# RWKV products of a hybrid layer regrouped by tile shape: y in two blocks, the solve's heads alternating over two PSUM tiles, the low-rank products as 64-row tiles

## The chip, the core and the metric

The kernel runs on one core of a Trainium2 chip. The metric is device time in microseconds (us) from one execution of the whole program. Three runs of the kernel before took 2709.77, 2721.66 and 2725.01 us; their median is 2721.66 us.

The engines are named as in the profile: PE multiplies matrices, PEld is its weight load, DVE is the vector engine, ACT the scalar engine, POOL the third elementwise engine, SP issues most transfers. PE multiplies a stationary operand (the weights, K rows by M columns) with a moving one (K rows by N columns). A product that uses fewer than 128 rows or columns of the array addresses a part of it, a tile of 64x128, 128x64 or 64x64 (rows x columns of the array). This tile shape is what the change is about.

## What is computed

One step of a layer over 1024 prompt tokens and 8 sample sequences, all in float32: a half-step SwiGLU feed-forward, two token mixers side by side (S5 and RWKV-7), a gated merge, a second half-step feed-forward and a final norm. The change lies in the RWKV-7 mixer, whose recurrence is, for each of 8 heads with a 64 x 64 state:

```
w = -softplus(-(w0 + tanh(wd) @ w2)) - 0.5;  decay = exp(-exp(w))
a = sigmoid(a0 + ad @ a2);  g = sigmoid(gd) @ g2          # low-rank: w2, a2 are 64 x 512
sa = einsum('bhij,bhj->bhi', s, a_t)
s  = s * decay + sa * b_t + v_t * k_t;   y_t = einsum('bhij,bhj->bhi', s, r_t)
```

wd and ad are 64 features each, and stand in one 128-row tile (wad): wd in rows 0 to 63, ad in rows 64 to 127.

## The kernel before, in words

Activations lie with features in the partitions and the 1032 columns (tokens, then samples) in three chunks of 344. A dense product (`dense`, L144 to L155) is split into three: high weights by high input (L152), high by low (L153), low by high (L154), each 128 x 128 weights and 344 columns. These make up most of PE's work in the whole kernel; a *dense pass* below is one of them. Products of plain float32 operands (the RWKV ones) are run by the chip as two passes each, so 8 products show as x16 in the profile; transposes (L160) as one.

The RWKV mixer (`rw_run`, L1076) takes 16 steps: two halves of the heads, and for each 8 blocks of 128 tokens. A step handles two head pairs of two 64-token chunks, thus four pieces j of two heads each. Head 0 of a pair sits on partitions 0 to 63, head 1 on 64 to 127 (`HS`). The stages of several steps overlap:

- `rw_prep`, five steps ahead: the low-rank products (L846), decay products on DVE, norms of the keys (L869). Here w2 and a2 stand in a zero-padded weight tile (`wa2`, two blocks of 512 columns, cleared on POOL at L776), so that one 128-row product per block takes only its own 64 rows of wad. Four products write one PSUM tile `sv`.
- `rw_solve`, three steps ahead: products of rows a, r with rows b, k (L917), 64 rows by 128 columns, four for head 0 into one `sv` tile, then four for head 1 into another. ACT and DVE read them out; then a 15-step substitution on DVE and a round trip through DRAM give the inverses of 16 x 16 blocks.
- `rw_quad`, one step ahead: transposes (L160), the bonus (L985) and five sets of 64x64 products (L997) that make the whole inverse.
- `rw_chain`: the recurrence itself. For each chunk c: L1023 (128x64), a copy on ACT, L1028 (64x64), two copies on ACT, L1033 (128x64), then DVE's new state (L1037), and the outputs y: for each of two pieces, two products of full height (L1041, 128x64), then two of 64 rows (L1043, 64x64) that are added to them.
- `rw_tail`: group norm and gate (L1064, 64x64; L1071, 128x128).

Pool `sv` has two PSUM slots, `qd` two, `ch` and `y` one each. A new tile of a pool waits until the tile that held its slot has been read. Beside these stages stand dense products of lower priority: the last three RWKV tiles and the gate tiles (`gate_tiles`, 72 dense passes each), which fill PE between the RWKV products. A scheduler merges them at build time into one fixed order on each engine, and each engine keeps that order. I call the piece of PE's order from the first L846 to the last L1071 *the stage*; after it come the rest of the gate tiles, the S5 gate (`glu_tile`), and the sample step (`rw_sample_vectors`, L1116, whose low-rank products are L1134, in pool `sm` with one slot).

Of the kernel before, what the change touches and what calls it, by code (L numbers as in the profile page):

```python
# [22 lines left out]
P = 128  # L23
D = 1024
KD = D // P
NP = 1024            # prompt tokens
NB = 8               # sample sequences
T = NP + NB          # columns
CH = T // 3          # column chunk (one PSUM bank)
LP = NP - 2 * CH     # prompt columns in the last chunk  # L30
# [11 lines left out]
def host_consts():  # L42
    """Identity, ones and masks; they depend on shapes alone."""
    r = np.arange(P)[:, None]
    c = np.arange(P)[None, :]
    c64 = np.arange(64)[None, :]
    m = r % 64
    up = lambda k: (((c64 >> k) - (m >> k)) == 1) & ((c64 >> (k + 1)) == (m >> (k + 1)))
    d = {
        "ident": r == c,  # L50
        "ones": np.ones((P, P)),
        "bones": r // 64 == c // 64,
        "su": r % 64 < c64,
        "ui": r % 64 <= c64,
        "up": np.concatenate([up(4), up(5)], axis=1),
        "i64": m == c64,
    }
    cf = np.concatenate([d[n].astype(np.float32) for n, _ in CF], axis=1)
    return np.ascontiguousarray(cf)
# [6 lines left out]
class Net:  # L66
# [51 lines left out]
    def split(self, hi, lo, src):  # L118
        """hi + lo = src exactly, both with 12 significant bits."""
# [4 lines left out]
    def wload(self, *srcs, pool=None):  # L124
        """One weight unit of at most 1024 columns as (hi, lo); srcs stack along the middle."""
# [14 lines left out]
    def wcols(self, w, j, n=P):  # L140
        """Column block j of w[(k p), f] as [p, k, n]."""
        return self.wload(w[:, j * n:(j + 1) * n].rearrange("(k p) f -> p k f", p=P))

    def dense(self, terms, c, cols=None):  # L144
        """terms: list of (wh, wl, xh, xl) with [K,128] and [K,cols]; returns PSUM."""
# [11 lines left out]
    def tr(self, out, in_):  # L157
        """out[M, K] = in_[K, M] transposed through the tensor engine."""
# [31 lines left out]
    def ada_steps(self, strips, pool):  # L190
        """Modulation columns of up to four 512-wide strips, side by side in the array; one step per k."""
# [24 lines left out]
    def norm_params(self, q, ks):  # L216
        """a = g (1 + scale) of norm q for the feature tiles ks."""
# [16 lines left out]
    def rsqrt(self, pt, scale, eps_col, pool, floor=None, n=CH, m=P, tmp=None):  # L234
        """1/sqrt(scale * pt + eps) (or of max(pt, floor)), refined by one Newton step."""
# [30 lines left out]
    def norm_apply(self, h, q, c, rs, xh, xl, pool):  # L266
        """One chunk of xh + xl = modulate(rmsnorm(h)) for norm q."""
# [23 lines left out]
    def norm_steps(self, h, q, pool, params=True):  # L291
        """scale(c, tag) and apply(c, xh, xl) of norm q, to be called chunk by chunk."""
# [9 lines left out]
    def resid(self, h, hin, pt, g, d, c):  # L302
        """h[d] = hin[d] + pt * g over one chunk."""
# [12 lines left out]
    def ffn(self, h, q, w1, w3, w2, xh, xl, gp, groups, hooks=None, wp2=None, wide=None):  # L316
        """h += gate * (silu(x w1) * (x w3)) w2 for the hidden tiles of some groups.

        wide: the order of a group's steps: "Hc.e" the hidden products of a chunk, "Oc" its output.
        """  # L320
# [39 lines left out]
    def load_x(self, h, g, pool):  # L360
        """Token tiles 3 g .. 3 g + 2 (the last group ends with the samples), transposed into h."""
# [24 lines left out]
    def final_out(self, h, c, pool, gf):  # L386
        """rmsnorm(h) * g_final for one chunk of tokens, turned token-major first."""
# [28 lines left out]
    def exp_small(self, out, x, pool, n):  # L416
        """exp(x) by range reduction and a polynomial (fp32 accuracy)."""
# [42 lines left out]
    def cmul(self, ore, oim, are, aim, bre, bim, t1, eng=None):  # L460
        """(ore, oim) = a * b; outputs must not alias inputs."""
# [9 lines left out]
    def s5_prep(self, sp):  # L471
        """Discretised parameters; the wide ones go to DRAM scratch by quarters of 8 groups."""
# [9 lines left out]
        # [(g2 n), gp] views of lam_re, lam_im and log_dt  # L482
# [30 lines left out]
        # k = (lam_bar - 1) / lam  # L513
# [15 lines left out]
        # powers lam_bar^tau, tau = 0..8, and the same reversed (7 - s)  # L529
# [12 lines left out]
        # bb[(g2 n), gp, c]  # L542
# [7 lines left out]
        # C as [(g2 n), gp, c]  # L550
# [14 lines left out]
        for g in range(16):  # L565
            nc.sync.dma_start(self.sK[:, 2 * g:2 * g + 2, 0:112], zer)
            # lam^(7-s) bb -> transposed
# [12 lines left out]
            # C lam^tau, sign folded into the imaginary part  # L580
# [6 lines left out]
            # K_tau[c, c']  # L587
# [10 lines left out]
            # e^{i 8 ang q}, q = 0..127  # L598
# [13 lines left out]
    def s5_quarter(self, qd, X, Xs, us, Z, h0, zs, dbc, pool, tag):  # L612
# [53 lines left out]
        # sample states: lam_bar h0 + bb u  # L666
# [8 lines left out]
        # outputs; one PSUM bank per parity of the group, as the parities use different row tiles  # L675
# [30 lines left out]
    def s5_mix(self, X, usT, zout, pool, tag="mm"):  # L706
        """X [128 q, 32 g, 8 s, 16 c] chunk-major inputs, usT [128, 4, 8]; zout(ct, tile) gets z transposed."""
# [12 lines left out]
        # sample rows, once as the first and once as the last token of a chunk  # L720
# [29 lines left out]
        # states out  # L750
# [11 lines left out]
    def rw_init(self, rows, keep, tag):  # L762
        """Per-feature vectors and low-rank weights."""
# [11 lines left out]
        wa2 = self.t(keep, [P, 2, 512], "rw_wa2")  # L775
        nc.gpsimd.memset(wa2, 0.0)  # L776
        nc.sync.dma_start(wa2[0:64, 0, :], i["rwkv_w2"])
        nc.sync.dma_start(wa2[64:128, 1, :], i["rwkv_a2"])
# [4 lines left out]
    def rw_clear(self, pool):  # L783
        """Zeros around the diagonal blocks of the inverses' scratches."""
# [8 lines left out]
    def rw_lora(self, wad, gd):  # L793
        """wad rows: 64 of wd, 64 of ad; gd: 128 rows (mixed, [128, T])."""
# [6 lines left out]
    def inv_half(x, h):  # L801
        """[64, 4, 64] view of head h; the heads of a scratch lie 4160 apart."""
# [3 lines left out]
    def inv_diag(x):  # L806
        """[32, 16, 16] view of the diagonal blocks of a scratch."""
        return x.rearrange("(q r) -> q r", r=1040)[:, 0:1024].rearrange("q (t s) -> q t s", s=64)[:, :, 0:16]

    def rw_decay(self, sw, tmp, r, exps):  # L810
        """exps(fm, fp, r): r (1 - t)^2 and r (1 + t)^2 are exp(-y), exp(y) for y = e^-0.5 sw and t = tanh(y/2)."""
# [3 lines left out]
        # 1 / (1 - t^2) = (1 + t^2)(1 + t^4)(1 + t^8)(1 + t^16), t < 0.295  # L815
# [13 lines left out]
    def rw_part(n):  # L829
        """Tokens of step n, and its two head pairs with their columns in the step's tiles."""  # L830
# [3 lines left out]
    def rw_prep(self, n, pool):  # L834
        """Decay products, normalised keys and the like for two chunks each of two head pairs."""
# [7 lines left out]
        pt = self.t(self.pp, [P, 2, 256], "sv")  # L843
        for p, ts in pairs:
            for z in range(2):
                nc.tensor.matmul(pt[:, z, ts], self.wa2[:, z, p * P:(p + 1) * P], self.wad[:, tok], start=True, stop=True)  # L846
        sw, b = new("sw"), new("pb", 2)
        for p, ts in pairs:
            nc.scalar.activation(sw[:, ts], pt[:, 0, ts], AF.Sigmoid, bias=col("w0", p))
        for p, ts in pairs:  # L850
            nc.scalar.activation(b[:, ts], pt[:, 1, ts], AF.Sigmoid, bias=col("a0", p))
# [27 lines left out]
    def rw_solve(self, n, q, pool):  # L879
        """Products of the rows a, r with the rows b, k of four chunks, and the inverses of I - A's 16-blocks.  # L880

        The state is carried without the decay of its last chunk, which a and r take up.  Head h's feature rows
        sit on its own half of the partitions with b's token rows; k's and v's token rows sit on the other.
        """
# [29 lines left out]
        for h, (hs, op) in enumerate(zip(HS, opp)):  # L914
            pm = self.t(self.pp, [P, 4, 2, 64], "sv")
            for j in range(4):
                nc.tensor.matmul(pm[:, j].rearrange("p a b -> p (a b)"), bk[hs, j],  # L917
                                 R[hs, j].rearrange("p a b -> p (a b)"), start=True, stop=True)
            nc.scalar.copy(At[hs], pm[hs, :, 0])
# [3 lines left out]
        # the 16 x 16 diagonal blocks, one per partition  # L923
# [28 lines left out]
    def rw_quad(self, n, q, sv, pool):  # L952
        """b, k and v with their tokens in the rows, the bonus, and the whole inverse."""
# [6 lines left out]
        # v of each head in the columns of the other half, next to columns that nothing reads  # L960
# [18 lines left out]
        # bonus  # L979
# [8 lines left out]
        # (I - A)^-1 = X P1 P2 from the inverse X of the diagonal blocks, with P1 = I + A1 X and P2 = I + A2 X P1 for  # L988
        # the blocks A1 next to them and A2 below; Y is the transpose
# [19 lines left out]
    def rw_chain(self, m, nxt, pool):  # L1009
        """The recurrence over two chunks of two head pairs; the state after each goes into the next one's operand."""  # L1010
# [6 lines left out]
        for c in range(2):  # L1017
# [21 lines left out]
            for a, j in js:  # L1039
                for h, hs, op in hh:  # L1040
                    mm(py[hs, 0, j], W[:, j, 1, h], SUV[:, j, h, 1], start=True, stop=False)  # L1041
                for h, hs, op in hh:
                    mm(py[hs, 0, j], rs[hs, j], SUV[hs, j, h, 0], start=False, stop=True)  # L1043
        return py

    def rw_tail(self, n, py, bon, pool):
        """Group norm, bonus and output gate of a step; py has the tokens of both heads in its rows."""
# [28 lines left out]
    def rw_run(self, pool):  # L1076
        """All head pairs, two at a time, two chunks a step, the stages of successive steps overlapped."""
# [38 lines left out]
    def rw_sample_vectors(self, pool, tag="sv"):  # L1116
        """Vectors of the samples' step, as [128, 8 samples, 4 head pairs] and as rows (sample, head) in DRAM."""
# [476 lines left out]
```

## Time and profile before

| | |
|---|---|
| runs | 2709.77, 2721.66, 2725.01 us |
| profiled execution | 2725.0 us, the span alone (the slowest of the three runs) |
| PE, PEld, DVE, ACT, POOL busy | 97%, 90%, 56%, 30%, 17% of the span |
| the stage, 1183 to 1649 us | PE busy 447.7, DVE busy 403.1 of 466 us |
| 1286 to 1552 us, its even part | PE busy 258.2, DVE busy 243.6 of 266 us |

How to read it: PE's busy time is modelled from start times, and a pass's record is longer than its place in the stream (a dense pass has a record of 0.32 us and the next one starts 0.16 us later). So what a product costs on PE is read from the differences of start times in the list in order of time. Rows of that list merge equal passes that follow each other: start, time from first start to last end, engine, line, operation, tiles, rows*columns of the array, operand shape, count.

### The profile page before, as it was taken

To read this page: it belongs to the slowest core of one execution; us is meant where nothing else is said; L and a number is where in the kernel's file an instruction comes from. 1 tells how busy PE (TensorE), PEld (TensorE's weight loads), DVE (VectorE), ACT (ScalarE), POOL (GpSimd) and SP (SyncE) were. 2 spreads that over 40 slices of the span, in tenths; PEclk is the share of its full clock that TensorE was granted. 3 is DMA by queue.
4 is the path that set the end of the run, shared out by engine and by line. 5 is a ranking of instruction groups with operands and counts; after the bars stand their busy time and mean duration, and the time that the engine had idled before them with its cause. 6 is when DMAs were issued, how large, how long until landed. Compare 5 with 4: busy or idle time off the path is not lost. (4 is left out here: it accounts for less than half of the span.)

```text
span 2725.0 us, 46727 instructions
## 1 busy us (share of the span) xinstructions
PE 2635.2 (97%) x18175; PEld 2454.6 (90%) x18175; DVE 1521.9 (56%) x4140; ACT 804.8 (30%) x1574; POOL 464.3 (17%) x1123
## 2 busy tenths in 40 slices
PE   7999999999999899999999999899899999999998
PEld 4799999999999898888888889899899999999998
DVE  4533446555555715559989973667854444444435
ACT  4311111111113412256666743221521111111113
POOL 2200003776002300022322210410410000000001
PEclk9999999999999997889999999899899999999999
DMA  7443341222122212333333327543211111111101
GB/s 258 114 139 111 123 128 55 63 66 69 60 68 94 79 54 84 88 105 81 82 79 79 86 64 212 171 120 105 66 55 47 47 47 47 47 47 47 48 24 63
DMA packets 301041, 233.20 MB, mean 86 GB/s; under 512 B 77778, under 2 KB 264947, under 8 KB 300820
## 3 DMA queue, kind: packets, MB, share of 16 engines
q1 hardware_dynamic: 298002, 224.04, 27.9%
q0 software_dynamic: 1920, 5.27, 0.5%
q8 instruction: 143, 2.34, 0.4%
q10 hardware_dynamic: 898, 0.91, 0.1%
q14 instruction: 78, 0.64, 0.1%
HBM read 186.23 MB, written 43.92 MB: 84 GB/s over the span
## 5 line engine op out<-in xcount | busy, mean ns | idle before, releaser
L152 PE MATMUL mm<-xa,wh 128*128 128x344 f32 x2064 | 677.9, 330 | 8.2 <-ACT xa L282 5.6
L154 PE MATMUL mm<-xa,wl 128*128 128x344 f32 x2064 | 674.2, 327 | 3.0 <-DVE wl L122 3.0
L153 PE MATMUL mm<-xb,wh 128*128 128x344 f32 x1848 | 604.0, 327 | 6.2 <-DVE xb L279 2.4
L153 PE MATMUL mm<-xa,wh 128*128 128x344 f32 x1368 | 442.6, 324 | 3.9 <-DVE xa L279 3.1
L121 ACT CAST wh<-wr 128x1024 fp32r<-128x1024 f32 (+1 forms) x190 | 194.6, 1030 | 792.4 <-PE mm L153 695.7
L152 PEld LDWEIGHTS mm<-xa,wh 128*128 128x128 f32 x2064 | 393.7, 191 | 38.5 <-issue 17.3
L307 DVE SCALAR_TENSOR_TENSOR h<-mm,modG,h 128x344 f32<-128x344 f32 (+1 forms) x624 | 351.6, 571 | 126.0 <-PE mm L154 108.7
L154 PEld LDWEIGHTS mm<-xa,wl 128*128 128x128 f32 x2064 | 393.8, 191 | 9.9 <-DVE wl L122 3.5
L152 PE MATMUL mm<-xb,wh 128*128 128x344 f32 x1152 | 371.7, 324 | 5.2 <-ACT xb L121 2.8
L154 PE MATMUL mm<-xb,wl 128*128 128x344 f32 x1152 | 371.1, 323 | 0.0
L153 PEld LDWEIGHTS mm<-xb,wh 128*128 128x128 f32 x1848 | 352.2, 191 | 16.1 <-DVE xb L279 4.7
L122 DVE TENSOR_TENSOR wl<-wr,wh 128x1024 fp32r<-128x1024 f32 (+1 forms) x190 | 230.7, 1214 | 223.3 <-ACT wh L121 218.6
L152 PE MATMUL mm<-gh,wh 128*128 128x344 f32 x1056 | 340.1, 322 | 2.1 <-DVE h L307 1.7
L153 PE MATMUL mm<-gl,wh 128*128 128x344 f32 x1056 | 337.9, 320 | 0.0
L154 PE MATMUL mm<-gh,wl 128*128 128x344 f32 x1056 | 337.9, 320 | 0.0
L328 DVE TENSOR_TENSOR silu<-silu,mm 128x344 f32<-128x344 f32 x132 | 67.5, 511 | 473.8 <-PE mm L154 424.6
L153 PEld LDWEIGHTS mm<-xa,wh 128*128 128x128 f32 x1368 | 260.9, 191 | 5.8 <-DVE xa L279 4.0
L152 PEld LDWEIGHTS mm<-xb,wh 128*128 128x128 f32 x1152 | 219.2, 191 | 7.2 <-ACT xb L282 3.2
L154 PEld LDWEIGHTS mm<-xb,wl 128*128 128x128 f32 x1152 | 219.2, 190 | 0.0
L152 PEld LDWEIGHTS mm<-gh,wh 128*128 128x128 f32 x1056 | 198.7, 188 | 7.5 <-ACT wh L121 2.5
L154 PEld LDWEIGHTS mm<-gh,wl 128*128 128x128 f32 x1056 | 198.7, 188 | 0.2
L153 PEld LDWEIGHTS mm<-gl,wh 128*128 128x128 f32 x1056 | 198.7, 188 | 0.1
(506 smaller groups left out, 3344.9 us busy)
## 6 DMA issues: line engine op xcount, KB each, us to landing
wr<-ffn_w SPq DMA_DIRECT2D x132, 512.0 KB
wada<-w_ada SPq DMA_DIRECT2D x144, 256.0 KB
wr<-w_in SPq DMA_DIRECT2D x34, 512.0 KB
sGate<-gate SPq DMA_DIRECT2D x48, 172.0 KB
gate<-sGate SPq DMA_DIRECT2D x48, 172.0 KB
sMix<-gate SPq DMA_DIRECT2D x36, 172.0 KB
sH<-h SPq DMA_DIRECT2D x8, 516.0 KB
h<-sH SPq DMA_DIRECT2D x8, 516.0 KB
```

Source lines behind the costliest of these rows:

```text
L121: nc.scalar.copy(hi, src)
L122: nc.vector.tensor_sub(lo, src, hi.bitcast(F32))
L152: nc.tensor.matmul(pt, wh, xh[:, cols], start=q == 0, stop=False)
L153: nc.tensor.matmul(pt, wh, xl[:, cols], start=False, stop=False)
L154: nc.tensor.matmul(pt, wl, xh[:, cols], start=False, stop=q == last)
L307: nc.vector.scalar_tensor_tensor(h[d][:, c0:c0 + np_], pt[:, :np_], g[:, d, 0:1], hin[d][:, c0:c0 + np_], op0=ALU.mult, op1=ALU.add)
L328: nc.vector.tensor_mul(s, s, p3)
```

## The change

Three regroupings, and comments removed (which shifts line numbers: L846 becomes L845, L869 L868, L917 L916, L1043 L1045, L1134 L1136).

- y: for each chunk first all four products of full height (L1041), then all four of 64 rows. Only the very first of a step sets the start flag; the others find their columns cleared.
- The solve: two `sv` tiles are taken at once, and the products alternate head 0, head 1.
- Low-rank: w2 and a2 stand one above the other in one 128 x 512 tile, without zeros. The products become 64-row ones, for w from rows 0 to 63 into one `sv` tile, for a from rows 64 to 127 into a second. In the sample step likewise, where pool `sm` has one slot for both.

```diff
-        wa2 = self.t(keep, [P, 2, 512], "rw_wa2")
-        nc.gpsimd.memset(wa2, 0.0)
-        nc.sync.dma_start(wa2[0:64, 0, :], i["rwkv_w2"])
-        nc.sync.dma_start(wa2[64:128, 1, :], i["rwkv_a2"])
+        wa2 = self.t(keep, [P, 512], "rw_wa2")
+        nc.sync.dma_start(wa2[0:64, :], i["rwkv_w2"])
+        nc.sync.dma_start(wa2[64:128, :], i["rwkv_a2"])
...
-        pt = self.t(self.pp, [P, 2, 256], "sv")
+        pts = [self.t(self.pp, [P, 256], "sv") for _ in HS]
         for p, ts in pairs:
-            for z in range(2):
-                nc.tensor.matmul(pt[:, z, ts], self.wa2[:, z, p * P:(p + 1) * P], self.wad[:, tok], start=True, stop=True)
+            for pt, hs in zip(pts, HS):
+                nc.tensor.matmul(pt[:, ts], self.wa2[hs, p * P:(p + 1) * P], self.wad[hs, tok], start=True, stop=True)
...
-        for h, (hs, op) in enumerate(zip(HS, opp)):
-            pm = self.t(self.pp, [P, 4, 2, 64], "sv")
-            for j in range(4):
+        pms = [self.t(self.pp, [P, 4, 2, 64], "sv") for _ in HS]
+        for j in range(4):
+            for pm, hs in zip(pms, HS):
                 nc.tensor.matmul(pm[:, j].rearrange("p a b -> p (a b)"), bk[hs, j],
                                  R[hs, j].rearrange("p a b -> p (a b)"), start=True, stop=True)
+        for h, (pm, hs, op) in enumerate(zip(pms, HS, opp)):
             nc.scalar.copy(At[hs], pm[hs, :, 0])
...
             for a, j in js:
                 for h, hs, op in hh:
-                    mm(py[hs, 0, j], W[:, j, 1, h], SUV[:, j, h, 1], start=True, stop=False)
+                    mm(py[hs, 0, j], W[:, j, 1, h], SUV[:, j, h, 1], start=c == 0 and a == 0, stop=False,
+                       skip_group_check=True)
+            for a, j in js:
                 for h, hs, op in hh:
-                    mm(py[hs, 0, j], rs[hs, j], SUV[hs, j, h, 0], start=False, stop=True)
+                    mm(py[hs, 0, j], rs[hs, j], SUV[hs, j, h, 0], start=False, stop=True, skip_group_check=True)
...
-        pt = ps([P, 2, 4, NB])
-        for p in range(4):
-            pc = slice(p * P, (p + 1) * P)
-            for z in range(2):
-                nc.tensor.matmul(pt[:, z, p], self.wa2[:, z, pc], self.wad[:, smp], start=True, stop=True)
         perm = lambda x: x.rearrange("p a b -> p b a")
-        v.tensor_add(sw, perm(pt[:, 0]), bc("w0"))
-        v.tensor_add(b, perm(pt[:, 1]), bc("a0"))
+        for hs, dst, off in zip(HS, (sw, b), ("w0", "a0")):
+            pt = ps([P, 4, NB])
+            for p in range(4):
+                nc.tensor.matmul(pt[:, p], self.wa2[hs, p * P:(p + 1) * P], self.wad[hs, smp], start=True, stop=True)
+            v.tensor_add(dst, perm(pt), bc(off))
```

The scheduler's order changes with it. Three places on PE, each in the middle of the stage; a row is line, operation, output<-operands, output shape, and how many such products follow each other.

One chunk's outputs y with the recurrence product before them (L1033), before:

```order
L1033 MATMUL ch_14632<-SUV_14237,WS_14230 64x64 x4
L1041 MATMUL y_14631<-SUV_14237,W_13745 64x64
L1043 MATMUL y_14631<-SUV_14237,rs_13754 64x64 x2
L1041 MATMUL y_14631<-SUV_14237,W_13745 64x64 x2
L1043 MATMUL y_14631<-SUV_14237,rs_13754 64x64 x2
```

and after:

```order
L1041 MATMUL y_14974<-SUV_14576,W_14080 64x64
L1033 MATMUL ch_14975<-SUV_14576,WS_14569 64x64 x4
L1041 MATMUL y_14974<-SUV_14576,W_14080 64x64 x3
L1045 MATMUL y_14974<-SUV_14576,rs_14089 64x64 x4
L153 MATMUL mm_17840<-xb_166,wh_17835 128x344
```

Two blocks of one tile shape each stand where four stood.

The low-rank products of one step, before:

```order
L1028 MATMUL ch_13322<-x_2024_13327,Y_1955_12943 64x64 x4
L154 MATMUL mm_17403<-xa_152,wl_17371 128x344
L152 MATMUL mm_17403<-xa_153,wh_17370 128x344
L846 MATMUL sv_13175<-wad_9647,rw_wa_1488_9875 128x128 x4
L153 MATMUL mm_17403<-xb_161,wh_17370 128x344
```

and after (the same step):

```order
L985 MATMUL qd_13268<-rk_13265,cf_58 128x256
L845 MATMUL sv_13180<-wad_9647,rw_wa_1488_9875 128x128 x2
L152 MATMUL mm_17418<-xa_152,wh_17385 128x344
L153 MATMUL mm_17418<-xb_160,wh_17385 128x344
L154 MATMUL mm_17418<-xa_152,wl_17386 128x344
L152 MATMUL mm_17418<-xa_153,wh_17385 128x344
L845 MATMUL sv_13181<-wad_9647,rw_wa_1488_9875 128x128 x2
L1028 MATMUL ch_13328<-x_2031_13333,Y_1961_12948 64x64 x4
```

The two halves (sv_13180 from rows 0 to 63, sv_13181 from rows 64 to 127) do not alternate: they stand apart, with other products between them.

The solves of two steps, after. First one that alternates, then one whose heads stand apart:

```order
L1045 MATMUL y_13983<-SUV_13590,rs_13105 64x64 x4
L916 MATMUL sv_14094<-R_14079,bk_14083 128x128
L916 MATMUL sv_14095<-R_14079,bk_14083 128x128
L916 MATMUL sv_14094<-R_14079,bk_14083 128x128
L916 MATMUL sv_14095<-R_14079,bk_14083 128x128
L916 MATMUL sv_14094<-R_14079,bk_14083 128x128
L916 MATMUL sv_14095<-R_14079,bk_14083 128x128
L997 MATMUL qd_13963<-Ys_13494,P_2143_13928 64x64 x8
L916 MATMUL sv_14094<-R_14079,bk_14083 128x128
L916 MATMUL sv_14095<-R_14079,bk_14083 128x128
```

```order
L1108 MATMUL ch_15068<-cf_58,So_14973 64x64 x4
L916 MATMUL sv_15095<-R_15080,bk_15084 128x128 x4
L1023 MATMUL ch_15313<-SUV_14904,W_14408 64x64 x2
L916 MATMUL sv_15096<-R_15080,bk_15084 128x128 x4
L1023 MATMUL ch_15313<-SUV_14904,W_14408 64x64 x2
```

Before, a solve had one head's four products and then the other's, whole or cut in two or three. Counted over the whole order: of 16 solves after, seven have their heads apart as in the second piece (with at most a few products cut off), the others alternate wholly or in part; of 32 low-rank groups, one alternates (the first step's) and 31 are of one half alone.

## Rows read from the trace of the kernel before

**Rows 1.** The page: span, and busy time of each engine.

```profile
span 2725.0 us, 46727 instructions
PE 2635.2 (97%) x18175; PEld 2454.6 (90%) x18175; DVE 1521.9 (56%) x4140; ACT 804.8 (30%) x1574; POOL 464.3 (17%) x1123
```

**Rows 2.** Busy time by stretches: us, busy (instructions) by engine, granted clock, DMA.

```profile
core 0: us, PE busy (x) PEld busy (x) DVE busy (x) ACT busy (x) POOL busy (x), PEclk, DMA share, GB/s
1183.00:1649.00 466.00, 447.71 (x4680) 381.25 (x4680) 403.14 (x1553) 288.23 (x615) 115.43 (x174) 0.98 0.34 83
1286.00:1552.00 266.00, 258.21 (x2827) 217.10 (x2827) 243.59 (x956) 176.27 (x380) 71.08 (x113) 1.00 0.34 82
1180.00:1200.00 20.00, 17.23 (x103) 16.15 (x102) 10.32 (x44) 14.41 (x25) 1.88 (x8) 0.91 0.48 145
1750.00:1770.00 20.00, 14.05 (x66) 13.44 (x65) 11.63 (x15) 3.50 (x6) 8.06 (x10) 0.77 0.55 168
```

**Rows 3.** PE's waits, 1200 to 1650 us: total, times, longest.

```profile
PE ch L1023 <- DVE SUV L1037: 4.0, 7, 1.2
PE qd L997 <- DVE qx L939: 3.7, 2, 2.9
```

**Rows 4.** PE in order of time: dense passes around one run of 64x64.

```profile
1480.61 0.32 PE L154 MATMUL mm<-xa,wl 128*128 128x344 f32 x1
1480.86 0.68 PE L1064 MATMUL y<-cf,t_y 64*64 64x64 f32 x16
1481.47 0.43 PE L152 MATMUL mm<-xa,wh 128*128 128x344 f32 x1
1481.74 0.32 PE L153 MATMUL mm<-xb,wh 128*128 128x344 f32 x1
1481.89 0.32 PE L154 MATMUL mm<-xa,wl 128*128 128x344 f32 x1
...
1492.07 0.32 PE L154 MATMUL mm<-xa,wl 128*128 128x344 f32 x1
...
1494.75 0.32 PE L153 MATMUL mm<-xb,wh 128*128 128x344 f32 x1
```

**Rows 5.** PE in order of time: outputs y of one chunk.

```profile
1486.30 0.34 PE L1041 MATMUL y<-SUV,W 128*64 128x64 f32 x4
1486.57 0.33 PE L1043 MATMUL y<-SUV,rs 64*64 64x64 f32 x4
1486.83 1.16 PE L917 MATMUL sv<-R,bk 64*128 64x128 f32 x10
```

**Rows 6.** PE in order of time: runs of 64x128, of one half and of both.

```profile
1231.19 1.16 PE L917 MATMUL sv<-R,bk 64*128 64x128 f32 x8
1232.27 0.43 PE L153 MATMUL mm<-xb,wh 128*128 128x344 f32 x1
...
1355.86 0.71 PE L917 MATMUL sv<-R,bk 64*128 64x128 f32 x4
1356.50 0.55 PE L160 MATMUL qd<-cf,bk 128*128 128x128 f32 x3
...
1562.78 1.04 PE L917 MATMUL sv<-R,bk 64*128 64x128 f32 x10
1563.75 0.34 PE L1041 MATMUL y<-SUV,W 128*64 128x64 f32 x4
```

**Rows 7.** PE in order of time: low-rank products between dense passes.

```profile
1233.01 1.05 PE L846 MATMUL sv<-wad,rw_wa 128*128 128x128 f32 x8
1233.82 0.40 PE L154 MATMUL mm<-xa,wl 128*128 128x344 f32 x1
```

**Rows 8.** PE in order of time: the sample step's products.

```profile
1700.65 1.84 PE L1134 MATMUL sm<-wad,rw_wa 128*128 128x8 f32 x16
1712.17 0.38 PE L1144 MATMUL sm<-sm,cf 128*128 128x32 f32 x2 [4.20 <-DVE sm L1142]
```

**Rows 9.** DVE in order of time: the first addition that reads them.

```profile
1704.10 0.18 DVE L1136 TENSOR_TENSOR sm<-sm,rw_vec 128x32 f32<-128x32 f32 x1
```

More of the change, by code (lines that the diff above doesn't have):

```diff
@@ L842, in rw_prep @@
             nc.sync.dma_start(kf[:, ts], self.mix_src(p, 1, tok))
-        pt = self.t(self.pp, [P, 2, 256], "sv")
+        pts = [self.t(self.pp, [P, 256], "sv") for _ in HS]
         for p, ts in pairs:
-            for z in range(2):
-                nc.tensor.matmul(pt[:, z, ts], self.wa2[:, z, p * P:(p + 1) * P], self.wad[:, tok], start=True, stop=True)
+            for pt, hs in zip(pts, HS):
+                nc.tensor.matmul(pt[:, ts], self.wa2[hs, p * P:(p + 1) * P], self.wad[hs, tok], start=True, stop=True)
         sw, b = new("sw"), new("pb", 2)
         for p, ts in pairs:
-            nc.scalar.activation(sw[:, ts], pt[:, 0, ts], AF.Sigmoid, bias=col("w0", p))
+            nc.scalar.activation(sw[:, ts], pts[0][:, ts], AF.Sigmoid, bias=col("w0", p))
         for p, ts in pairs:
-            nc.scalar.activation(b[:, ts], pt[:, 1, ts], AF.Sigmoid, bias=col("a0", p))
+            nc.scalar.activation(b[:, ts], pts[1][:, ts], AF.Sigmoid, bias=col("a0", p))
         Dp = self.t(pool, [P, 4, 65], "Dp", bufs=2)
```

## The prediction

> **What bounds the kernel now.** I read the page first: PE is busy for 97% of the span, DVE for 56% [rows 1]. So time is what PE's stream of products takes, and a change counts by what it puts into that stream or takes out of it. But the change lies in one stage, so I read the stretches next. In the stage (466 us) PE is busy 447.7 and DVE 403.1 us, and in its even part (266 us) PE 258.2 and DVE 243.6, which is 92% [rows 2]. There the two engines are nearly level; what is taken off PE alone need not come out as time. The list of waits says the same from the other side: PE's longest sums are waits for DVE, but they are small, 4.0 us in 7 waits for L1037 [rows 3]. PE's own busy time says little about what a product costs, so the prices come from start times in the list in order of time.
>
> **Prices.** A dense pass follows the last after 0.158 us (2.68 us for the 17 steps from 1492.07 to 1494.75) [rows 4]. When PE goes over to another tile shape, it pays twice. From dense to the 64x64 products of L1064 it is 0.25 us instead of 0.158; after them the first dense pass is followed after 0.27 instead of 0.158 [rows 4]. So a stretch of 128x128 costs 0.09 + 0.11 = 0.20 us for being one more. A run of four 64-wide passes takes 0.27 or 0.26 us [rows 5], one of 16 takes 0.61 [rows 4]: 0.029 for each pass more, and 0.15 fixed. A run of 64x128 takes 0.64 us with four passes of one half, 1.08 with eight [rows 6]: 0.11 a pass and 0.20 fixed. These fixed costs are what the regrouping is about.
>
> Two halves of 64x128 do run at once where they stand near each other: ten passes, six of head 0 and four of head 1, took 0.97 us [rows 6], which is 0.20 fixed and 7 steps of 0.11 instead of 10. The Trainium skill says the same in TensorE: Matmul & The Clock Gate, Part 3 (packing small matmuls): tiles in different row groups overlap, and a set costs about one product and some ns for each further tile. By that rule alone every low-rank product and every product of the solve would be halved, and the sum would be that of the first rival below; by the order that PE has been given, few of them meet.
>
> **The change part by part.** I count stretches of equal tile shape in PE's order of the stage: 512 before, 498 after. By the shape they begin: 64x64 and 128x64 go from 301 to 246, 64x128 from 37 to 72, 128x128 from 174 to 180.
>
> - y: each chunk loses two of its four runs. 16 steps x 2 chunks x 2 x 0.15 = -9.6 us. The passes stay 512 (256 of each kind). Nothing covers this: PE issues them one after the other.
> - The other 64-wide runs are cut up more often by the new order, 9 runs more: +1.3 us.
> - Low-rank: before, the eight passes of a step (0.81 us to the next start [rows 7], 0.10 each) have the shape of the dense ones beside them and pay no fixed cost there. After, 32 runs of 64x128, each of one half but the first step's: 32 x 0.20 = +6.4; the passes cost the same, save four that overlap, -0.4. Sum +6.0 us.
> - The solve: 40 runs instead of 37, +0.6. Its 256 passes take about 215 steps before (heads meet by chance, as in [rows 6]) and 200 after: -15 x 0.11 = -1.7. Sum -1.1 us.
> - Six stretches of 128x128 more, +1.2 us.
>
> PE's work changes by -9.6 + 1.3 + 6.0 - 1.1 + 1.2 = -2.2 us. Nearly all that y gives, the low-rank products take.
>
> Moved work: the stage holds 72 dense passes less (one gate tile), which come after it: 72 x 0.158 = 11.4 us out of the stage and back behind it. That is nothing if PE sets the time at both places. In the stage PE thus has 13.6 us less to do, and DVE only one weight split less. Whether the stage gets shorter by all of that depends on DVE. If it follows PE, PE's idle time stays as it is: 0. If DVE's pace holds, the stage stays as long: +13.6 us of new PE waits. Below 0 is possible too: at the stage's start PE idles more (17.2 us busy of 20 [rows 2]), and there the new order puts some more runs, which idle time would cover; I allow -4. I take +4, nearer to the PE end, since PE's busy share in the even part (97%) is above DVE's (92%) [rows 2] and the shortening also takes away part of DVE's waits for PE.
>
> Two `sv` slots: rw_prep now takes both at once, and its second tile waits until DVE has read the second tile of the solve before it. That is what drives the halves apart in the order. It holds up nothing else: the solve that needs these results comes two steps later. I count 0 and leave it within the +13.6.
>
> The sample step: pool `sm` has one slot, so the second half's four products wait for DVE's addition of the first half. PE keeps its order, so all dense passes behind them wait too. Before, the products end at 1702.5 (1700.65 + 1.84) and DVE adds at 1704.10, 1.6 us later, since it stands behind the gates' multiplications [rows 8, 9]. In the new order three dense passes (0.5 us) cover that: a wait of some 1.1 us. Then L1144 has 24 dense passes before it instead of 34, so 1.6 us less cover for its wait of 4.2 us [rows 8]; but part of that chain has begun earlier. I take +2, from 0 (the addition comes at once) to +5.
>
> The memset on POOL that goes was hidden (POOL is busy 17% [rows 1]): 0. The start flags of y cost nothing: same passes.
>
> **Sum.** -2.2 + 4 + 2 = +3.8 us. The profiled execution took 2725.0 us, its span alone, and is the slowest of the three; the same difference on the median gives 2721.7 + 3.8 = **2725.5 us**. The bounds add up to -6 and +16.4. A change of under 0.5% (13.6 us; the three runs lie 15 us apart) can't be told from none here, and I forecast such a one.
>
> **Rivals.**
>
> 1. *All pairs overlap as the source has them.* Solve: 16 x (0.20 + 8 x 0.11) = 17.3 us against 37 x 0.20 + 215 x 0.11 = 31.1 now, -13.8; low-rank 16 x (0.20 + 4 x 0.11) + 16 x 0.20 for the dense stretches they cut = 13.4 against 128 x 0.11 = 14.1, -0.7; y -9.6. Sum -24: 2698 us. For it: the overlap in [rows 6]. Against it: seven solves and 31 of 32 low-rank groups stand apart in the order, with products of other shapes between them. 8%. It is also what the packing rule of the Trainium skill, named above, would give (TensorE: Matmul & The Clock Gate, Part 3).
> 2. *PE sets the pace throughout.* Waits as before, the sample step within its cover: -2.2, 2719.5 us. For it: PE 97% busy, waits small [rows 2, 3]. 15%.
> 3. *DVE holds the stage at its length*, slower. The stage shrinks by nothing, and the gate tile that left it is paid behind it: -2.2 + 13.6 = +11.4, and the sample step +2. The idle time that PE gets in larger pieces lowers its clock: over 1180 to 1200 us, where PE waited, the granted clock is 0.91, so 0.09 x 20 = 1.8 us lost; over 1750 to 1770 it is 0.77, 4.6 us lost [rows 2]. Two such dips more, 3.2 each, +6.4. Sum +19.8: 2741.5 us. For it: DVE at 92% in the even part [rows 2]. Against it: DVE still has 8% of its own waits, part of them for PE. It decides from the point where DVE's share in the stage after is at about 95%. 19%.
>
> My forecast has the other 58%.
>
> **How the numbers follow.** Below 2708 (faster by over 0.5%) lie the first rival but for a bit (7%) and tails of the second and the forecast (4%): 11%. Above 2735.3 lie three quarters of the third rival (14%) and 5% of the forecast: 19%. Within: 70%. The range leaves out the first rival and the upper part of the third: 2704 to 2743 us, which takes in -6 and +16.4 and a few us of the runs' own spread. The forecast's own range is 2716 to 2738.
>
> **What would show it.** In the profile after: y as runs of eight passes, each some 0.38 us to the next start; low-rank runs of four passes, 0.64 us each, with dense passes between; solves partly at 1.1 us for 16 passes, partly at 1.08 for eight; the stage shorter by 5 to 13 us, with a DVE share above 92% in its even part; behind the second half of the sample's products no long idle time, before it a wait for DVE of 1 to 2 us. I am wrong if the low-rank halves run at once after all, if the stage is as long as before, if a wait of several us appears where there was none (the inverses of L997 are the likeliest place, since some steps now have fewer passes ahead of them), or if a run's fixed cost is other than 0.15 to 0.20 us.

## The result, and the profile after

The changed kernel takes 2743.66 us (median of 4 runs, 2742.93 to 2751.32) against 2721.40 us before (a fourth run, of 2721.14 us, is in that median). The ratio is 1.010, with an interval of 1.008 to 1.013: slower by about 1%. The prediction was 2725.5 us with a range up to 2743, and its forecast was a change of under 0.5%, which can't be told from none. It was wrong: the time lies 0.7 us above the range and 18 above the forecast.

The page after, in answer to [rows 1], hardly shows why: span and busy shares read almost the same.

```profile
span 2741.2 us, 46728 instructions
PE 2643.7 (96%) x18175; PEld 2452.6 (89%) x18175; DVE 1518.9 (55%) x4140; ACT 802.4 (29%) x1570; POOL 461.8 (17%) x1122
```

The stretches do show it. These are the same columns as in [rows 2]: first the stage, then its even part, then three pieces of it.

```profile
core 0: us, PE busy (x) PEld busy (x) DVE busy (x) ACT busy (x) POOL busy (x), PEclk, DMA share, GB/s
1178.90:1657.10 478.20, 454.51 (x4602) 380.08 (x4602) 399.32 (x1549) 282.58 (x607) 114.08 (x172) 0.93 0.31 78
1282.00:1548.00 266.00, 252.18 (x2614) 206.89 (x2612) 228.13 (x892) 164.19 (x359) 67.90 (x108) 0.90 0.31 75
1440.00:1457.00 17.00, 15.89 (x129) 12.55 (x129) 11.48 (x48) 8.99 (x21) 2.53 (x3) 0.70 0.19 51
1473.00:1487.00 14.00, 14.00 (x93) 10.58 (x91) 6.98 (x24) 7.25 (x20) 2.29 (x3) 0.51 0.20 47
1498.00:1531.00 33.00, 29.87 (x277) 23.70 (x277) 28.52 (x115) 18.46 (x41) 8.31 (x14) 0.64 0.26 61
```

The stage got 12.2 us longer (478.2 against 466.0) although 72 dense passes left it. Read column by column:

- Clock: the mean granted clock fell from 0.98 to 0.93. At half level for part of the time, the stage loses (1 - mean) x length: 9.3 us before, 33.5 us after, so +24.2. This is an estimate that takes PE to be busy while its clock is low; the pieces above bear that out (14.00 of 14 us, 29.87 of 33).
- PE's waits (length less PE busy): 18.3 before, 23.7 after, so +5.4.
- What is left is PE's work at full clock: 438.4 before, 421.0 after, so -17.4. Of this 11.4 us are the 72 passes that moved behind the stage. The rest, -6.0, answers to the -2.2 of the prediction; a clock with two digits leaves some 2.4 us open on each side, so the two can't be told apart.

DVE's share of the even part fell from 92% to 86% (228.13 of 266). DVE did not hold the stage at its length.

Behind the stage the 72 passes are paid. In the two profiled executions the stage begins 4.1 us earlier after (1178.9 against 1183.0) and the span ends 16.2 us later, so what lies behind the stage costs 8.1 us more: 11.4 for the passes, and 3.3 less for the rest.

The waits, in answer to [rows 3] and in the same stretch (us in total, times, longest):

```profile
PE ch L1023 <- DVE SUV L1037: 7.9, 6, 2.3
PE sv L868 <- ACT pt L866: 2.4, 1, 2.4
PE sv L916 <- DVE bk L898: 2.3, 2, 1.9
...
PE sv L845 <- DVE W L921: 1.3, 2, 1.0
```

The third and the fourth are waits for operands or for an `sv` slot, in front of products that the recurrence needs only some steps later. How they come to matter is seen in PE's list in order of time (start, duration, operation, and in brackets the idle time before it), in the worst piece. It covers the second half of step 8 and step 9 of the recurrence.

```profile
1497.55 0.45 PE L1023 MATMUL ch<-SUV,W 128*64 128x64 f32 x8 [1.26 <-DVE SUV L1037]
...
1501.54 0.70 PE L985 MATMUL qd<-rk,cf 128*128 128x256 f32 x2
1502.17 0.45 PE L1023 MATMUL ch<-SUV,W 128*64 128x64 f32 x8
1503.65 0.68 PE L845 MATMUL sv<-wad,rw_wa 64*128 64x128 f32 x4 [1.03 <-DVE W L921]
1504.26 0.45 PE L1028 MATMUL ch<-x,Y 64*64 64x64 f32 x8
...
1507.63 0.70 PE L1023 MATMUL ch<-SUV,W 128*64 128x64 f32 x8 [1.14 <-DVE SUV L1037]
1508.25 1.11 PE L997 MATMUL qd<-Xs,Au 64*64 64x64 f32 x14
1509.69 0.66 PE L154 MATMUL mm<-xa,wl 128*128 128x344 f32 x1 [0.32 <-DVE wl L122]
1510.14 0.49 PE L152 MATMUL mm<-xa,wh 128*128 128x344 f32 x1
...
1516.99 1.12 PE L997 MATMUL qd<-P,X 64*64 64x64 f32 x16
...
1531.83 0.32 PE L153 MATMUL mm<-xb,wh 128*128 128x344 f32 x1
1531.99 0.32 PE L154 MATMUL mm<-xa,wl 128*128 128x344 f32 x1
```

For 12 us from 1497.6 there is no dense pass at all. So each wait of the recurrence is bare: PE has nothing else to run. At 1503.65 a low-rank product stands in the queue in front of L1028 and waits 1.03 us until DVE has read the solve's tile out of the slot; L1028, which the recurrence needs, waits behind it. Then, from about 1507.5, the clock is at half level: a run of 16 passes of 64x64 takes 1.12 us there, against 0.68 in [rows 4], and it comes back only at 1531, when dense passes again follow one another (1531.83 to 1531.99 is 0.16 us).

The dense passes in steps 8 and 9 alone, each from the step's first L1023 to that of step 10; first before, then after (the columns are us, PE busy in these passes with their number, clock):

```profile
1476.30:1525.60 49.30, 26.14 (x124) 1.00 0.35 85
```

```profile
1471.40:1533.60 62.20, 17.76 (x67) 0.70 0.24 57
```

57 passes fewer, 9.0 us at 0.158 each, and yet 12.9 us longer.

Not all of this lies where dense passes are missing. After 1341 us the clock is low in three spells: 1442.5 to 1453, 1473 to 1487 and 1507.5 to 1531.5, at 0.50 to 0.51. The last, half of that time, begins in the stretch without dense passes. The second lies in the first half of step 8, which has 42 dense passes (47 before); the first comes among dense passes, behind this wait:

```profile
1441.11 0.45 PE L1023 MATMUL ch<-SUV,W 128*64 128x64 f32 x8 [1.91 <-DVE SUV L1037]
```

### The profile page after: what moved, and what is told of

Same layout as the page of the kernel before. It is cut to its first block, busy times and chain, and to the rows that moved or that the text cites. A ratio compares the mean times of both kernels' runs of the same rounds, so it can differ in the third digit from the quotient of the medians.

```text
span 2741.2 us, 46728 instructions
## 1 busy us (share of the span) xinstructions
PE 2643.7 (96%) x18175; PEld 2452.6 (89%) x18175; DVE 1518.9 (55%) x4140; ACT 802.4 (29%) x1570; POOL 461.8 (17%) x1122
```

## The experiments

Three theories stood at the start, a fourth came with the fifth run. **Theory 1**: the low-rank products in two slots change PE's order so that some steps lose their dense passes; PE waits there and its clock falls. **Theory 2**: runs of 64x128 cost far more than 0.20 us. **Theory 3**: DVE holds the stage at its length. **Theory 4**: two slots taken at once hold up DVE and PE whatever the order.

All runs, with the stage's row of the stretches of each (stage, clock and waits are those of one profiled execution; its time can lie some us off the median):

| run | median us | ratio (interval) | stage us | its clock | PE's waits |
|---|---|---|---|---|---|
| before | 2721.40 | 1 | 466.0 | 0.98 | 18.3 |
| after | 2743.66 | 1.010 (1.008 to 1.013) | 478.2 | 0.93 | 23.7 |
| e1, y alone | 2710.89 | 0.997 (0.995 to 0.998) | 450.7 | 1.00 | 19.9 |
| e2, y and solve | 2715.01 | 0.999 (0.998 to 1.000) | 457.9 | 0.95 | 27.2 |
| e3, low-rank alone | 2747.44 | 1.010 (1.007 to 1.013) | 491.0 | 0.91 | 18.2 |
| e4, two tiles, 128 rows | 2734.85 | 1.006 (1.004 to 1.009) | 464.7 | 0.94 | 25.1 |
| e5, after, order held | 2721.05 | 1.000 (0.999 to 1.001) | 466.1 | 0.97 | 20.9 |
| e6, y and solve, order held | 2709.65 | 0.995 (0.994 to 0.997) | 450.5 | 0.99 | 19.3 |
| e7, y, source lines swapped | 2812.11 | 1.033 (1.031 to 1.036) | 461.9 | 0.80 | 86.5 |
| e8, after with filler | 2737.85 | 1.007 (1.005 to 1.008) | 470.2 | 0.95 | 21.9 |
| e9, e5 with a second slot | 2720.14 | 1.001 (1.000 to 1.003) | 466.9 | 0.96 | 20.4 |
| e10, low-rank, order held | 2729.23 | 1.004 (1.002 to 1.006) | 474.7 | 0.96 | 16.3 |

Measured beside e1 to e4 the kernel before had a median of 2719.14, beside e5 to e8 2720.58, beside e9 and e10 2716.81; after was measured beside the 2721.40 of the first row. The ratios go by these, so a difference between runs of two such groups is rough by a few us.

**e1, y alone.** Only y's loops of the diff are kept; the order is before's but for y.

> The kernel before with y regrouped alone; solve and low-rank products as before. PE's order is that of before but for y: 1202 dense passes in the stage, 448 stretches of equal shape instead of 512. Theory 1 (the order: the low-rank part makes the scheduler leave a stretch of some 20 us of the stage almost without dense passes, PE waits there and its clock falls): no such stretch here, so 64 runs x 0.15 = -9.6 us, about 2712. Theory 2 (the 64x128 runs of the low-rank products cost far more than the 0.20 us each that I took): the same, 2712, since none is added. Theory 3 (DVE holds the stage at its length, so PE's saving is not taken): no change, 2721.

It came to -8.3 us. The price of 0.15 us for each of 64 runs (-9.6) about holds, and the time follows PE: Theory 3 falls, since DVE's work and the dense passes are as before.

**e2, y and the solve in turns over two tiles.** The two loops of the diff, low-rank as before.

> The kernel before with y regrouped and the solve alternating; low-rank products as before. 440 stretches of equal shape, 1138 dense passes in the stage (64 fewer, 10.1 us that come behind it), the poorest stretch of dense passes some 12 us. Theory 1: no long stretch without dense passes, PE's work falls by 13.7 us, about 2708. Theory 2: 2708 to 2711. Theory 3: the stage stays as long, the 64 passes are paid behind it, about 2731.

A miss: 7 us above Theory 1's figure, 4 above Theory 2's range and 16 under Theory 3's. Instead of a gain over e1 it lost 4.1. The stage has 64 dense passes fewer, the clock is 0.95, waits are 27.2 instead of 19.9. So a cost that comes with order is likely there already; e6 tests it.

**e3, the low-rank products alone.** Two lines of the edit:

```
- pt = self.t(self.pp, [P, 2, 256], "sv")
+ pts = [self.t(self.pp, [P, 256], "sv") for _ in HS]
```

> The kernel before with the low-rank products as 64-row tiles in two PSUM tiles alone; y and solve as before. 559 stretches of equal shape, 1130 dense passes in the stage, one stretch of 20 us almost without dense passes. PE's work rises by 10.4 us by my prices. Theory 1: the same poor stretch as in the changed kernel, low clock there, so the changed kernel's time and some 12 us more for y and the solve, 2750 to 2756. Theory 2: the excess of the changed kernel (some 24 us) comes with the 64x128 runs, so 2721 + 10 + 24 = 2755 too. Theory 3: 2721 + 11 behind the stage, 2732.

+28.3 us, the whole loss of the change and more; 2747.44 is 3 us under Theory 1's range, 8 under Theory 2's figure and 15 above Theory 3's. From 1503 to 1538 us its clock is 0.51 with PE busy for 33.8 of 35 us.

**e4, two tiles but 128 rows.** The changed kernel with each engine's order as it is, but the products zero-padded to 128 rows again; so only the tile shape goes. The edit against the changed kernel, shortened:

```
- self.wa2[hs, p * P:(p + 1) * P], self.wad[hs, tok]
+ self.wa2[:, z, p * P:(p + 1) * P], self.wad[:, tok]
```

> The changed kernel, but the low-rank products are again 128-row ones against the zero-padded weights, each still into its own of two PSUM tiles (prompt and sample). Every engine keeps the order of the changed kernel; only the tile shape of 72 products differs, so 36 stretches of equal shape fewer. Theory 1 (the order): the poor stretch and the low clock stay, only the price of the shapes goes, -7 us: about 2737. Theory 2 (the 64x128 runs): all of the excess goes, about 2712. Theory 3: as the changed kernel, 2743.

8.8 us less than after by the medians (by the ratios, 1.006 against 1.010, 11; the two intervals overlap, so the size is rough), and 2 us under Theory 1's figure. That is what the 64-row shape costs in this order, with what it does to the clock (0.94 against 0.93; the prediction had +6.0), and it leaves 15.7 us over before, 24 over e1, that the shape does not explain. Theory 2 falls.

**e5, the changed kernel with PE's order held.** All operations, tiles and slots are those of the change. Added are only rules of order: the recurrence's products L1023, L1028 and L1033 of each half step may not be issued before as many dense passes as stood ahead of them in the kernel before. Shortened:

```
+ for key, n in PACE.items():          # counts read from before's order
+     tc.add_manual_dep(CH1[key].ins, DL[base + n - 1].ins.name, NoSync)
```

> The changed kernel with every product, tile and slot as it is; only PE's order is held: in each step the recurrence's first products (px, pu, ps) may not be issued before as many dense passes as stood ahead of them in the kernel before. So each step gets back its dense filler (steps 8 and 9 have 50 passes in the half step in which the change leaves 0). Theory 1 (order: a stretch without dense passes, PE waits there, its clock falls) expects the stage's priced work to be 4 us under before's, waits of PE and low-clock time as before (about 20 us each), so 2712 to 2720 us, 25 to 30 below the changed kernel. Theory 2 (runs of 64x128 cost far more than 0.20 us) expects 2735 or more, since 62 of the 71 runs stay. Theory 4 (two slots taken at once hold up DVE and PE whatever the order) expects 2735 to 2743.

2721.05, level with before and 22.6 under after (by the ratios, 1.000 against 1.010, 28). It ended 1 us above Theory 1's range and 14 below that of the others; Theories 2 and 4 fall. In the profiled stages, against after, the dense passes that are back cost 11.4 us, the clock takes 19.5 less and the waits 2.8 less; the sum is -10.9, and the stage is 12.1 shorter. Steps 8 and 9 have their passes again:

```profile
1477.10:1525.50 48.40, 26.04 (x126) 1.00 0.33 80
```

None of the three late spells of after is left: to the stage's end the clock is 1.00 in e5 from 1344 us on, as it is before from 1270 us on (e5 first, then before, all engines):

```profile
1344.00:1643.50 299.50, 294.27 (x3449) 246.20 (x3448) 259.40 (x1002) 195.45 (x416) 66.93 (x109) 1.00 0.33 81
```

```profile
1270.00:1649.00 379.00, 368.63 (x4165) 308.11 (x4162) 329.97 (x1281) 235.94 (x506) 87.89 (x139) 1.00 0.32 78
```

Why it is not the 4 us under before that prices give is not settled; seen are the stage's clock of 0.97 and a wait of 6.1 us in the sample step, to which e9 comes back.

**e6, y and the solve in turns, order held.**

> Only y and the solve as in the change, low-rank products as before, with the same hold on PE's order as in the paced changed kernel. The solve in turns had cost 4 us against y alone, with 44 us of low clock in the stage. Theory 1 expects that to go: low clock under 15 us, and 2707 to 2713 us, level with y alone (2710.9). Theory 4 expects 2713 to 2718, as without the hold.

In the range, and 5.4 us under e2 with the same operations. Its clock is 0.99. It has the lowest median of all, 0.5% under before; its interval overlaps that of e1.

**e7, order alone.** e1 with two statements of the step loop exchanged:

```
+ if s + 5 < 16: q[s + 5] = self.rw_prep(s + 5, pool)
  if 0 <= s + 3 < 16: sv[s + 3] = self.rw_solve(s + 3, q[s + 3], pool)
- if s + 5 < 16: q[s + 5] = self.rw_prep(s + 5, pool)
```

> Order alone: y's products regrouped, all else as before, but in each step the source writes the low-rank part of step s+5 ahead of the solve of step s+3. No tile shape and no slot differs from the kernel with y alone; the scheduler now puts no dense pass at all into steps 2 to 11, and they come behind the stage. Theory 1 expects PE to wait in these steps and its clock to be at half level for most of them: over 100 us of low clock, 40 us or more slower than y alone, 2750 us or more. If the place of the dense passes did not matter (Theories 2 and 4), 2711 us.

+101 us on e1, with the same products, more than twice the 40 that Theory 1 asked for at least. The stretches of e7, of the stage and of the steps without dense passes, and two of the waits there:

```profile
1184.30:1646.20 461.90, 375.37 (x4032) 313.56 (x4030) 390.05 (x1541) 242.70 (x559) 109.92 (x172) 0.80 0.27 63
1308.00:1575.00 267.00, 192.39 (x2169) 155.57 (x2170) 230.47 (x936) 128.01 (x313) 67.74 (x112) 0.67 0.22 47
```

```profile
PE ch L1028 <- ACT x L1025: 16.1, 9, 3.1
PE sv L846 <- DVE W L921: 6.5, 4, 3.6
```

645 dense passes (101.9 us at 0.158) have left the stage, and it is 11 us longer than e1's. Waits take 66.6 us more. The clock takes at most (1 - 0.80) x 461.9 = 92.4; here PE also waits while the clock is low, which costs nothing more, and over its busy 375.4 us alone the estimate is 75. So taking dense passes out of the stage did not shorten it, and behind it 88.1 us are paid: e7's span ends 1165.0 us after its stage, e1's 1076.9. The exchange also changes which product takes an `sv` slot first, so not only dense passes moved.

**e8, filler.** The changed kernel with 48 products more whose results are thrown away, in steps 8 and 9. Shortened:

```
+ if (self.step, c) in ((8, 1), (9, 0)):
+     for _ in range(12): nc.tensor.matmul(<py's second half>, fx[:, 0:P], fx[:, 0:256])
```

> The changed kernel with 48 passes that compute nothing used (128x128 weights, 256 columns, same type as the dense passes) put into the half steps 8 and 9 that have no dense pass, behind px and pu; up to there PE's order is the changed kernel's, and behind it the scheduler moves some dense passes too. They add 48 x 0.115 = 5.5 us of work. Theory 1 expects the low clock from about 1497 us on to go (some 24 to 30 us of it) and with it 12 to 15 us: 5 to 10 us faster than the changed kernel, 2733 to 2739, in spite of the work added. If waits or something else sets the time there and not the missing passes: 2743 to 2749.

5.8 us faster, with more work, and in Theory 1's range; all four runs lie under all four of after. What was added, in PE's list, one of two such places:

```profile
1491.01 2.18 PE L1051 MATMUL y<-xa 128*128 128x256 f32 x16
1493.12 0.68 PE L997 MATMUL qd<-Y,Pm 64*64 64x64 f32 x16
1493.73 1.22 PE L1051 MATMUL y<-xa 128*128 128x256 f32 x8
1494.79 0.38 PE L160 MATMUL qd<-cf,bk 128*128 128x128 f32 x2
```

and the dense passes in steps 8 and 9 of e8 alone (after had 67 in 62.20 us, at a clock of 0.70):

```profile
1479.00:1533.20 54.20, 15.82 (x76) 0.97 0.31 71
```

The 24 passes here take 2.11 + 1.06 us, so 48 about 6.4 us; against after, some 12 us came back elsewhere. The filler can't be given all of it. The first of it is issued at 1491.01, and the piece ahead of it, in which after has its spell from 1473 to 1487 with the same products in the same order, kept full clock in e8:

```profile
1480.60:1491.00 10.40, 10.40 (x144) 8.22 (x141) 8.55 (x30) 7.59 (x20) 2.39 (x3) 1.00 0.32 68
```

So that spell went without the filler's help. What lies behind the filler is the other one: from 1499.8 to 1533.2 us e8's clock is 0.95, where after has 0.67 from 1497.5 to 1533.6. Over whole executions, the four of e8 have a granted clock of 0.968 to 0.972, the four of after 0.961 to 0.967.

**e9, a second slot for the sample step.** e5, with the second half's products in a slot of `mm`.

```
- pt = ps([P, 4, NB])
+ pt = self.t(self.pp, [P, 4, NB], tg)      # tg: "sm", then "mm"
```

> The changed kernel with PE's order held as in the paced one, and in the sample step the second half's four products go to a slot of pool mm instead of waiting for the one slot of sm. In the paced kernel these products waited 6.1 us for DVE's addition. If the slot is the reason, that wait goes and with it about 6 us: 2713 to 2717 us, against 2721 of the paced kernel; if another chain ends last there (the vectors' DMA, for which PE waits 5.4 us behind it), 2719 to 2722.

The slot is not the reason: 2720.14 lies where the second case was expected. The wait for the slot is gone, but L1144 waits 4.3 us for DVE behind it, where e5 had none, and L160 3.4 for a DMA (5.4 in e5). By the median 0.9 us under e5, by the ratios 0.1% above; nothing is shown to be gained.

**e10, the low-rank products alone, order held** (with e9's slot).

> Only the low-rank products as 64-row tiles in two slots (solve and y as before), PE's order held to before's dense filler, and the sample's second half in a slot of mm. Without the hold this cost 28 us. The prices of the prediction give +6.0 us for the 64-row shape (60 runs of 64x128 instead of 37) and 3 dense passes more in the stage. Theory 1 expects 2723 to 2730 us; Theory 2 (the shape itself is dear) or Theory 4 (two slots at once) 2740 or more.

2729.23 is within Theory 1's range, but before took 2716.81 beside it: the range stands for +2 to +9, and it came to +12.4 (by the interval 6.5 to 16), where e3 had +28.3. The two slots and a clock of 0.96 are in it, so that the shape alone is dearer than its price of 6.0 is not shown.

## Why the prediction was wrong

**The step that failed** is the pair "Moved work" and "Two `sv` slots". The prediction wrote that the 72 passes are "nothing if PE sets the time at both places", that the two slots "hold up nothing else", and took +4 for waits. It noted that the slots drive the halves apart in the order, but it followed only the halves and not the dense passes. And no term of its sum stands for the clock. The passes were not taken out evenly: by PE's order the second half of step 8 and the first half of step 9 went from 10 and 53 passes to none. The order by itself is worth 22.6 us (after less e5, which differ in nothing else). In place of the +4 stand, in the profiled stage, +5.4 of waits and +24.2 of clock. That the waits came near +4 is luck, since they were taken to come from DVE's pace. The prediction's own signs of being wrong came too: the stage, which was to be 5 to 13 us shorter, was 12.2 longer, and DVE's share in the even part was 86% and not above 92%.

That the order costs this is shown by e5 and e7. How it does so is shown in part: half of the low-clock time after 1341 us begins in the two half steps without dense passes, the other half lies elsewhere in the same order, and of it the spell from 1473 did not come in e8.

**The third rival** came closest in its time (2741.5) but not in its way. Its condition, DVE at 95%, did not come: DVE's share fell. So its nearness is luck. It did have two dips of the clock, 3.2 us each, from [rows 2]; the loss was of that kind but nearly four times as large (24.2 against 6.4). Rivals 1 and 2 did not come; the halves stand apart as said, and each of the 31 groups pays its own run.

**Point by point:**

- y, -9.6: about right, -8.3 (e1). In the profile after a run of eight takes 0.38 us to the next start, as said, in answer to [rows 5]; the low-rank run of four takes 0.64, in answer to [rows 7]:

```profile
1342.39 0.71 PE L845 MATMUL sv<-wad,rw_wa 64*128 64x128 f32 x4
1343.03 0.50 PE L997 MATMUL qd<-Xs,Au 64*64 64x64 f32 x9
...
1352.71 0.45 PE L1045 MATMUL y<-SUV,rs 64*64 64x64 f32 x8
1353.09 0.37 PE L916 MATMUL sv<-R,bk 64*128 64x128 f32 x1
```

- Low-rank, +6.0: the sign is right; 8.8 (e4) and 12.4 (e10) were measured, both rough and with some clock in them. [rows 7] is the cheapest place of before: beside 64-wide runs its groups of eight take 0.98 to 1.09 us and not 0.81.
- Solve, -1.1: with the order held e6 is 1.2 us under e1 by the medians, which agrees but can't be told from nothing; as built it is +4.1 (e2).
- Sample step, +2: wrong in the changed kernel. The wait of 4.20 us in [rows 8] is gone, and the new one for the slot does not come, since DVE adds at once (PE first, then DVE):

```profile
1723.77 1.06 PE L1136 MATMUL sm<-wad,rw_wa 64*128 64x8 f32 x8
1725.42 1.05 PE L1136 MATMUL sm<-wad,rw_wa 64*128 64x8 f32 x8
1730.30 0.30 PE L1144 MATMUL sm<-sm,cf 128*128 128x32 f32 x2
```

```profile
1724.86 0.19 DVE L1137 TENSOR_TENSOR sm<-sm,rw_vec 128x32 f32<-128x32 f32 x1 [0.40 <-PE sm L1136]
```

  But nothing is gained: the next wait, for a DMA, grew by as much (before first, then after). The two waits sum to 7.7 us before, 7.5 after, 11.5 in e5 and 7.7 in e9:

```profile
PE sm L160 <- DMA smo<-sS: 3.5, 1, 3.5
```

```profile
PE sm L160 <- DMA smo<-sS: 7.5, 1, 7.5
```

  In e5 the wait does come, and is longer than the bound of the prediction, because DVE's addition stands behind a multiplication of the gates that itself waits for a DMA (PE first, then DVE):

```profile
1700.90 1.88 PE L1136 MATMUL sm<-wad,rw_wa 64*128 64x8 f32 x8 [6.13 <-DVE sm L1137]
```

```profile
1700.22 0.52 DVE L1345 TENSOR_TENSOR gate<-gate,gate 128x344 f32<-128x344 f32 x1 [3.82 <-DMA gate<-sGate]
1700.66 0.18 DVE L1137 TENSOR_TENSOR sm<-sm,rw_vec 128x32 f32<-128x32 f32 x1
```

- The places named for a new wait: L997 was named, L1023 it was (4.0 to 7.9 us), and the waits are the smaller part.

What stays open: e2's order, which held e1's gain back, was put right as a whole (e6), not traced to one step; and e5's clock of 0.97 against before's 0.98, with spells between 1190 and 1345 us, was not looked into further. And when the clock falls in a given order is open.

## What to carry to other kernels

Where a long recurrence of small products runs with large products as filler, the filler's place is part of the cost: count the large products per step in the new order beside the old one before pricing an edit, and take it that a step that has none may run at a lower clock (0.67 over the 267 us of e7 that have almost none). Taking two slots of a pool at once (e2, e3), or exchanging two statements (e7), came with such moves. An order that is good can be held by rules of issue order when the operations change; here this was worth 22.6 us, and the best regrouping 8.3.

## What the runs showed of the hardware

- The clock fell without a long wait. From 1473 to 1487 us PE was busy for 14.00 of 14 us at a clock of 0.51, with 13 dense passes among the 93. What it did just before: the last dense pass of a series starts at 1469.23, and up to 1473.01 there are only small products and one wait of 0.41 us. But from 1428 to 1434 us, with one dense pass among 111 and no wait, the clock stayed at 1.00. And in e8 the same products in the same order, behind the same wait of 0.41 us, kept 1.00. So neither the mix nor the order settles by itself when the clock falls. The Trainium skill, in TensorE: Matmul & The Clock Gate, Part 1 (HAM oscillation — how this bites in real kernels), puts such falls down to long waits for DMA between groups of products, and counts the loss as half the time at the lower level. The second about agrees: in that spell a dense pass follows the last after 0.29 us, against 0.158. The first is not the only way, as no wait in the stretch of the waits above is longer than 2.4 us.

```profile
1478.31 0.49 PE L153 MATMUL mm<-xb,wh 128*128 128x344 f32 x1
1478.60 0.49 PE L154 MATMUL mm<-xa,wl 128*128 128x344 f32 x1
```

- Work added can go with a shorter time: the kernel with 6.4 us of products that nothing reads was 5.8 us faster (e8).
- A product that uses half the rows was dearer than the same one padded with zeros where its neighbours are full. Between dense passes at full clock a group of four takes 0.64 us to the next start after, and 0.36 to 0.47 in e4; one place of the order is shown, first after, then e4. Beside 64-wide runs it is 0.64 in both (1343.03 less 1342.39 after, 1345.59 less 1344.95 in e4).

```profile
1421.07 0.71 PE L845 MATMUL sv<-wad,rw_wa 64*128 64x128 f32 x4
1421.71 0.43 PE L153 MATMUL mm<-xb,wh 128*128 128x344 f32 x1
```

```profile
1423.63 0.60 PE L846 MATMUL sv<-wad,rw_wa 128*128 128x128 f32 x4
1423.99 0.41 PE L153 MATMUL mm<-xb,wh 128*128 128x344 f32 x1
```
